# A hybrid attention block on one core: x and ctx transposed unscaled as half rows land, 1/rms spread over partitions, first-stage order pinned

## The chip, the cores and the metric

The kernel runs on one core of a Trainium2 chip. The metric is the device time of one execution in microseconds, shown as the median of three runs. All arithmetic is float32; a matmul operand is split into a high part (a float32 rounded to the matmul's own format, fp32r) and a low part, the remainder, so that one product becomes three matmuls.

## The reference

One layer of a backbone block with 256 latent tokens (`x`) and 256 context tokens (`ctx`), width 2048. What matters here is its beginning:

```python
sh1, sc1, ... = split(silu(c) @ w_mod + b_mod, 6)      # for x, from c
csh1, csc1, ... = split(silu(c_ctx) @ w_mod + b_mod, 6)  # for ctx, from c_ctx
h  = rmsnorm(x,   g_attn) * (1 + sc1)  + sh1
hc = rmsnorm(ctx, g_attn) * (1 + csc1) + csh1
cq, ckv, kr, qn, kn, vn, f   = split_columns(h  @ w_in)
cq_c, ckv_c, kr_c, ...       = split_columns(hc @ w_in)
```

where `rmsnorm(x, g)` is `x / sqrt(mean(x*x) + eps) * g` along a token's 2048 channels. Behind it follow three groups of attention and mixing heads, an output projection, and a gated MLP with a depthwise convolution.

## The kernel before

**Layout.** Token rows arrive with tokens on the 128 partitions: four tiles `xt[0..3]` of 128 tokens by 2048 channels, two of `x` and two of `ctx`. The first stage wants channels on partitions: `xT[m]` holds four channel blocks of 128 (kt = 4m to 4m+3) by 512 tokens.

**The start (lines 286 to 302 and 359 to 366).** SP issues the four loads of x and ctx, one of 1 MB each, and then the stream of weights. ScalarE issues the small loads: `sa` (modulation inputs), `sm` (among others the identity matrix for transposes, and `c` for `c1`) and `rope`. ScalarE then makes `c1` from `sm`, squares each x tile and sums it (`ssx`); VectorE and GpSimd (POOL) make 1/rms from that (`rstd`, lines 102 to 106), and VectorE multiplies the tile by it (line 301). TensorE transposes the scaled tile, four 128 x 128 blocks into one PSUM bank (line 364), with the identity from `sm`; VectorE and ScalarE take turns in copying the banks to `xT` (line 365).

**The first stage (lines 309 to 375).** For each of the 16 channel blocks kt there are two pieces of TensorE work. The *mod product* (`mod1_mm`, 32 matmuls of 256 columns, line 318) computes shift and scale of that block for both streams from 2 MB of `w_mod` (two tiles `m`); `mod1_h` transposes its copy `part` (line 326), VectorE finishes shift and scale in three small steps (lines 330 to 332), and VectorE and ScalarE make the modulated `hx` and `hc` with high and low parts (lines 342 to 344). The *group product* (`g1`, 42 matmuls, lines 109 to 111) adds that block's contribution to seven accumulators, from block `wA`, of which each 896 KB tile serves two kt in four quarters. The loop runs mod product g, the first `G1_CUT` tiles of group product g-1, `mod1_h(g)`, and the rest of g-1.

**Weights.** `emit_dma` issues loads on SP in the order of the list `order` (per pair of kt: m, m, A, m, m); tiles come from a pool of 16 buffers of 8 KB a partition, shared with x, `xT` and the squares' scratch. `take` splits quarters of a weight tile ahead of their use: `split` (lines 120 to 124) is a cast on ScalarE for the high part and a subtraction on VectorE for the low part.

**What sets the order.** A scheduler places each engine's instructions when the program is built; on the chip an engine runs them in that order, each waiting for the semaphores of what it needs. `tc.issue_after(i)` forbids the scheduler to place what follows before instruction i. An SP load waits for one of eight DMA semaphores, so about eight loads can be out at a time.

The lines that fill the start are these:

```python
act.activation(junk, xt[t], AF.Square, accum_out=ssx[:, t : t + 1])
rstd(rx[:, t : t + 1], ssx[:, t : t + 1], D)
dve.tensor_scalar(xt[t], xt[t], rx[:, t : t + 1], None, ALU.mult)
...
pe.transpose(ps[:, k * P : (k + 1) * P], xt[t][:, kt * P : (kt + 1) * P], ident)
```

## Time and profile before

| | |
|---|---|
| median of 3 runs | 1277.77 us (1277.18 to 1279.66) |
| profiled execution, its own time | 1279.01 us |
| its span, first to last instruction | 1277.2 us |
| TensorE busy | 1243.7 us, 97% of the span |
| VectorE, ScalarE, POOL busy | 77%, 55%, 9% |
| mean granted TensorE clock | 0.997 of full speed |
| moved by DMA | 304.81 MB, 239 GB/s on average |

The span is a little shorter than the execution's own time, which holds what lies before the first and behind the last instruction. Busy time is the sum of an engine's instructions; TensorE's weight loads are counted apart. Lines are those of the kernel before; tile names stand without their buffer numbers.

### The profile page before, as it was taken

To read this page: it belongs to the slowest core of one execution; us is meant where nothing else is said; L and a number is where in the kernel's file an instruction comes from. 1 tells how busy PE (TensorE), PEld (TensorE's weight loads), DVE (VectorE), ACT (ScalarE), POOL (GpSimd) and SP (SyncE) were. 2 spreads that over 40 slices of the span, in tenths; PEclk is the share of its full clock that TensorE was granted. 3 is DMA by queue.
4 is the path that set the end of the run, shared out by engine and by line. 5 is a ranking of instruction groups with operands and counts; after the bars stand their busy time and mean duration, and the time that the engine had idled before them with its cause. 6 is when DMAs were issued, how large, how long until landed. Compare 5 with 4: busy or idle time off the path is not lost.

```text
span 1277.2 us, 19956 instructions
## 1 busy us (share of the span) xinstructions
PE 1243.7 (97%) x7536; PEld 1069.2 (84%) x7536; DVE 978.6 (77%) x1757; ACT 699.0 (55%) x1343; POOL 111.5 (9%) x177
## 2 busy tenths in 40 slices
PE   5999999999999999999999999999999999999996
PEld 4888879898787888999988878888888888888885
DVE  5444588999989788899989975777766677777785
ACT  5333323765555555576666544666654566556663
POOL 0000121111111002200121500000000000000000
PEclk9999999999999999999999999999999999999999
DMA  9998689677756977754767857544455645564531
GB/s 387 419 397 327 223 305 323 231 243 249 258 194 232 368 294 270 261 227 165 286 226 253 320 204 264 212 162 169 165 198 180 249 165 183 184 227 165 172 125 66
DMA packets 53648, 304.81 MB, mean 239 GB/s; under 512 B 6064, under 2 KB 7216, under 8 KB 26800
## 3 DMA queue, kind: packets, MB, share of 16 engines
q1 hardware_dynamic: 34256, 234.37, 49.7%
q0 software_dynamic: 18432, 67.12, 15.5%
q10 hardware_dynamic: 864, 2.05, 0.4%
q8 instruction: 59, 0.97, 0.3%
q14 instruction: 37, 0.30, 0.1%
HBM read 301.42 MB, written 2.10 MB: 238 GB/s over the span
## 4 chain that ended last, share of the span: by engine, by line
PE 90%; DMA 3%; DVE 3%; issue 1%; ACT 1%; POOL 0%; DVEq 0%; ACTq 0%; POOLq 0%
PE ps L834 21%; PE ps L109 16%; PE ps L110 15%; PE ps L111 15%; PE ps L835 11%; DMA wm<-in_wm_dram 3%; PE g L109 2%; PE ms L318 2%; PE g L110 2%; PE g L111 2%; DVE acc L236 1%; DVE hl L124 1%; PE ps L493 1%; PE ps L364 1%; DMA sm<-in_small_dram 1%
## 5 line engine op out<-in xcount | busy, mean ns | idle before, releaser
L123 ACT CAST hl<-raw 128x512 fp32r<-128x512 f32 (+2 forms) x732 | 444.0, 611 | 359.8 <-PE ps L111 191.1
L124 DVE TENSOR_TENSOR hl<-raw,hl 128x512 fp32r<-128x512 f32 (+2 forms) x732 | 485.8, 677 | 172.6 <-ACT hl L123 166.4
L834 PE MATMUL ps<-hn,hl 128*128 128x512 f32 x1152 | 404.3, 395 | 0.0
L835 PE MATMUL ps<-hn,hl 128*128 128x256 f32 x1152 | 323.4, 281 | 0.0
L834 PEld LDWEIGHTS ps<-hn,hl 128*128 128x128 f32 x1152 | 216.4, 188 | 51.2
L835 PEld LDWEIGHTS ps<-hn,hl 128*128 128x128 f32 x1152 | 217.1, 188 | 0.2
L236 DVE SCALAR_TENSOR_TENSOR acc<-wm,c,acc 128x1024 f32<-128x1024 f32 x120 | 153.6, 1280 | 8.7 <-DMA wm<-in_wm_dram 8.4
L110 PE MATMUL ps<-hl,act 128*128 128x512 f32 x344 | 135.7, 394 | 0.5 <-DVE hl L124 0.5
L109 PE MATMUL ps<-hl,act 128*128 128x512 f32 x344 | 135.2, 393 | 0.0
L111 PE MATMUL ps<-hl,act 128*128 128x512 f32 x344 | 135.2, 393 | 0.0
L221 POOL DMA_DIRECT2D wm<-in_wm_dram x128 | 68.3, 534 | 310.7 <-DVE acc L236 233.8
L110 PEld LDWEIGHTS ps<-hl,act 128*128 128x128 f32 x344 | 64.7, 188 | 15.9 <-DVE hl L124 1.5
L109 PEld LDWEIGHTS ps<-hl,act 128*128 128x128 f32 x344 | 64.6, 188 | 14.9
L111 PEld LDWEIGHTS ps<-hl,act 128*128 128x128 f32 x344 | 64.7, 188 | 14.6
L109 PE MATMUL ps<-h,hl 128*128 128x258 f32 x256 | 72.5, 283 | 0.0
L111 PE MATMUL ps<-h,hl 128*128 128x258 f32 x256 | 72.1, 282 | 0.0
L110 PE MATMUL ps<-h,hl 128*128 128x258 f32 x256 | 72.1, 282 | 0.0
L216 POOL COPY hold<-hl 128x1 f32<-128x1 f32 x36 | 36.0, 999 | 286.7 <-DVE hl L124 286.7
L109 PE MATMUL ps<-hl,mix 128*128 128x512 f32 x128 | 50.5, 394 | 0.0
L110 PE MATMUL ps<-hl,mix 128*128 128x512 f32 x128 | 50.1, 391 | 0.0
L111 PE MATMUL ps<-hl,mix 128*128 128x512 f32 x128 | 49.9, 390 | 0.0
L855 ACT ACTIVATE cv<-ps,sm 128x256 f32<-128x256 f32 x88 | 49.4, 564 | 0.5
(282 smaller groups left out, 2143.2 us busy)
## 6 DMA issues: line engine op xcount, KB each, us to landing
raw<-in_wup_dram SPq DMA_DIRECT2D x88, 1024.0 KB, 5.1
wm<-in_wm_dram POOLq DMA_DIRECT2D x128, 512.0 KB, 5.1
raw<-in_wdn_dram SPq DMA_DIRECT2D x44, 1024.0 KB, 4.9
raw<-in_wm_dram SPq DMA_DIRECT2D x32, 1024.0 KB, 14.4
raw<-in_wo_dram SPq DMA_DIRECT2D x16, 1024.0 KB, 9.9
raw<-in_wB_dram SPq DMA_DIRECT2D x10, 1024.0 KB, 7.4
raw<-in_wA_dram SPq DMA_DIRECT2D x8, 896.0 KB, 14.5
x<-in_x_dram SPq DMA_DIRECT2D x4, 1024.0 KB, 8.8
```

Source lines behind the costliest of these rows:

```text
L109: pe.matmul(ps, lH, rH, start=first, stop=False, skip_group_check=skip)
L110: pe.matmul(ps, lH, rL, start=False, stop=False, skip_group_check=skip)
L111: pe.matmul(ps, lL, rH, start=False, stop=last, skip_group_check=skip)
L123: act.copy(H, src)
L124: return dve.tensor_tensor(L, src, H.bitcast(F32), ALU.subtract).ins
L216: hold = pool.tensor_copy(tiny(1, "hold"), recent[0][:, 1, 0:1].bitcast(F32)).ins
L221: pool.dma_start(w, a["wm2"][blk * 16 + kt])
L236: dve.scalar_tensor_tensor(m2["a"], w, c1[:, kt : kt + 1], m2["a"], ALU.mult, ALU.add)
L318: pe.matmul(ms[r : r + 32, 0:256], cs[:, 8 * q + k, :], w[:, k, :], start=(q == 0 and k < 4), stop=(q == 1 and k >= 4), tile_position=(0, r))
L834: pe.matmul(ps, w[:, 0, k * P : (k + 1) * P], h[:, :, k, :], start=kt == 0, stop=False, skip_group_check=True)
L835: pe.matmul(ps[:, :SEQ], w[:, 1, k * P : (k + 1) * P], h[:, 0, k, :], start=False, stop=kt == KT - 1, skip_group_check=True)
L855: act.activation(t, ps[:, :SEQ], AF.Identity, bias=c[:, 3:4], scale=c[:, 1:2])
```

## The change

The parts, in the order of the diff:

- `G1_CUT` is 2 instead of 4: `mod1_h` stands behind two tiles of the group product before, not four.
- The identity for the transposes, `idt`, is made on POOL from ones, and no longer read from `sm`.
- The load of a `wA` tile is cut into halves by columns; the second half is issued behind the next second mod tile.
- The quarters 2 and 3 of `wA` block 0 are split only behind the newest `hx`.
- x and ctx are loaded in eight half rows (512 KB each), then the first five weight loads are issued.
- `x_in`: per half row a Square with its own sum, and two groups of four transposes of the unscaled tile; all 16 copies to `xT` are on VectorE. `sm` is loaded behind the last Square.
- `x_rms`: the two half sums are added, 1/rms is made for all four tiles at once, put on a diagonal, and spread over all partitions by a product with ones, behind the first mod product; ScalarE copies it to `rxb`.
- `mod1_h` multiplies the block of `xT` by `rxb`, behind the h32 of the block before.
- Mod products and mod transposes of later blocks are held behind the group product issued before them; `rope` and `c1` stand behind the first `hx`.

```diff
-N_A, G1_CUT = 7, 4
+N_A, G1_CUT = 7, 2
...
+    idt = const.tile([P, P], F32, name="idt")
+    pool.affine_select(idt, ones, [[1, P]], ALU.is_equal, 0.0, base=0, channel_multiplier=-1)
...
-        pe.matmul(ps, lL, rH, start=False, stop=last, skip_group_check=skip)
+        ins = pe.matmul(ps, lL, rH, start=False, stop=last, skip_group_check=skip).ins
         paced(3 * rH.shape[-1])
+        return ins
...
             raw = b8([P, 2048], s="raw")
-            last_dma[0] = sync.dma_start(raw[:, :w], a[name][idx]).ins
+            if key[0] == "A":
+                sync.dma_start(raw[:, : w // 2], a[name][idx, :, : w // 2])
+                late_half.append((raw[:, w // 2 : w], a[name][idx, :, w // 2 :]))
+            else:
+                last_dma[0] = sync.dma_start(raw[:, :w], a[name][idx]).ins
+                if late_half and key[0] == "m" and key[2] == 1:
+                    sync.dma_start(*late_half.pop())
             raws[key] = raw
...
-            ins = split(t[:, 0, :hs], t[:, 1, :hs], raws[k][:, o : o + hs])
+            with ExitStack() as held:
+                if k == ("A", 0) and q >= 2:
+                    held.enter_context(tc.issue_after(hx_made[-1]))
+                ins = split(t[:, 0, :hs], t[:, 1, :hs], raws[k][:, o : o + hs])
             hls[k, q] = recent[0] = t
             last_split[0] = ins
...
+    ssrx = const.tile([P, 16], F32, name="ssrx")
+    ssx, sst, rx = ssrx[:, 0:8], ssrx[:, 8:12], ssrx[:, 12:16]
     xt = []
     for t in range(4):
         x_ = b8([P, D], s="x")
-        sync.dma_start(x_, (a["x"] if t < 2 else a["ctx"])[(t % 2) * P : (t % 2 + 1) * P, :])
+        for h in range(2):
+            sync.dma_start(x_[:, h * 1024 : (h + 1) * 1024],
+                           (a["x"] if t < 2 else a["ctx"])[(t % 2) * P : (t % 2 + 1) * P, h * 1024 : (h + 1) * 1024])
         xt.append(x_)
-        if t == 0:
+    emit_dma(order.index(("m", 1, 1)))
+    hmade, hx_made, g1_last, m_mm = [], [], [], []
+
+    def x_in():
+
+        last = None
+        for t in range(4):
+            junk = b8([P, D], s="junk")
+            for h in range(2):
+                c = slice(h * 1024, (h + 1) * 1024)
+                last = act.activation(junk[:, c], xt[t][:, c], AF.Square, accum_out=ssx[:, 2 * t + h : 2 * t + h + 1]).ins
+                for m in (2 * h, 2 * h + 1):
+                    ps = bank()
+                    for k in range(4):
+                        kt = 4 * m + k
+                        pe.transpose(ps[:, k * P : (k + 1) * P], xt[t][:, kt * P : (kt + 1) * P], idt)
+                    dve.tensor_copy(xT[m][:, :, t * P : (t + 1) * P], ps.rearrange("p (k q) -> p k q", k=4))
+        with tc.issue_after(last):
             act.dma_start(sm, a["small"])
-    act.dma_start(rope, a["rope"])
-    for t in range(4):
-        junk = b8([P, D], s="junk")
-        act.activation(junk, xt[t], AF.Square, accum_out=ssx[:, t : t + 1])
-        rstd(rx[:, t : t + 1], ssx[:, t : t + 1], D)
-        dve.tensor_scalar(xt[t], xt[t], rx[:, t : t + 1], None, ALU.mult)
-    act.activation(c1, smv("c1"), AF.Silu)
+
+    rxb = b2(s="rxb")
+
+    def x_rms():
+        sv = ssx.rearrange("p (t h) -> p t h", h=2)
+        dve.tensor_tensor(sst, sv[:, :, 0], sv[:, :, 1], ALU.add)
+        rstd(rx, sst, D)
+        dgs = b2(s="dgx")
+        dve.tensor_tensor(dgs.rearrange("p (t q) -> p t q", t=4), idt.rearrange("p (o q) -> p o q", o=1).broadcast_to((P, 4, P)),
+                          rx.rearrange("p (t o) -> p t o", o=1).broadcast_to((P, 4, P)), ALU.mult)
+        ps = bank()
+        with tc.issue_after(m_mm[0]):
+            pe.matmul(ps, ones, dgs, start=True, stop=True)
+        return act.copy(rxb, ps).ins
 
 
     hx, hc = [None] * 4, [None] * 4
...
     def mod1_mm(g):
 
-        for q in range(2):
-            w = raw_tile(("m", g, q), 6)
-            w = w.rearrange("p (k n) -> p k n", k=8)
-            for k in range(8):
-                r = 32 * (k % 4)
-                pe.matmul(ms[r : r + 32, 0:256], cs[:, 8 * q + k, :], w[:, k, :], start=(q == 0 and k < 4),
-                          stop=(q == 1 and k >= 4), tile_position=(0, r))
+        with ExitStack() as held:
+            if g:
+                held.enter_context(tc.issue_after(g1_last[-1]))
+            for q in range(2):
+                w = raw_tile(("m", g, q), 6)
+                w = w.rearrange("p (k n) -> p k n", k=8)
+                for k in range(8):
+                    r = 32 * (k % 4)
+                    ins = pe.matmul(ms[r : r + 32, 0:256], cs[:, 8 * q + k, :], w[:, k, :], start=(q == 0 and k < 4),
+                                    stop=(q == 1 and k >= 4), tile_position=(0, r)).ins
+                m_mm.append(ins)
         sb = b1(s="part")
         act.copy(sb, ms[:, 0:256])
         return sb
 
     def mod1_h(kt, sb):
-        for s in range(2):
-            pe.transpose(ms[:, 256 + s * P : 256 + (s + 1) * P], sb[:, s * P : (s + 1) * P], ident)
+        with ExitStack() as held:
+            if kt:
+                held.enter_context(tc.issue_after(g1_last[-1]))
+            for s in range(2):
+                pe.transpose(ms[:, 256 + s * P : 256 + (s + 1) * P], sb[:, s * P : (s + 1) * P], idt)
         t = tiny(4, "mt")
         tv = t.rearrange("p (s j) -> p s j", s=2)
...
+        xk = xT[m][:, kt % 4, :]
+        with ExitStack() as held:
+            if kt:
+                held.enter_context(tc.issue_after(hmade[-1]))
+            dve.tensor_tensor(xk, xk, rxb, ALU.mult)
...
-            dve.tensor_scalar(h32, xs, A, B, ALU.mult, ALU.add)
-            act.activation(H, xs, AF.Identity, bias=B, scale=A)
+            hmade.append(dve.tensor_scalar(h32, xs, A, B, ALU.mult, ALU.add).ins)
+            hx_made.append(act.activation(H, xs, AF.Identity, bias=B, scale=A).ins)
             dve.tensor_tensor(L, h32, H.bitcast(F32), ALU.subtract)
...
-            mm3(accs[i][:, SEQ:], lH, lL, *hsl(hc, kt), first=False, last=(kt == KT - 1), skip=True)
-
-    for t in range(4):
-        for m in range(4):
-            ps = bank()
-            for k in range(4):
-                kt = 4 * m + k
-                pe.transpose(ps[:, k * P : (k + 1) * P], xt[t][:, kt * P : (kt + 1) * P], ident)
-            (act.copy if m % 2 else dve.tensor_copy)(xT[m][:, :, t * P : (t + 1) * P],
-                                                     ps.rearrange("p (k q) -> p k q", k=4))
+            g1_last.append(mm3(accs[i][:, SEQ:], lH, lL, *hsl(hc, kt), first=False, last=(kt == KT - 1), skip=True))
+
+    x_in()
+    sb0 = mod1_mm(0)
+    rx_made = x_rms()
     accs = [bank(f"g1_{i}") for i in range(N_A)]
     for g in range(KT):
+        if g == 0:
+            mod1_h(0, sb0)
+            continue
+        if g == 1:
+            g1(0, range(0, 4))
+            with tc.issue_after(hx_made[-1]):
+                act.dma_start(rope, a["rope"])
+                act.activation(c1, smv("c1"), AF.Silu)
         sb = mod1_mm(g)
-        if g:
-            g1(g - 1, range(0, G1_CUT))
+        n = 5 if g == 1 else G1_CUT
+        g1(g - 1, range(4 if g == 1 else 0, n))
         mod1_h(g, sb)
-        if g:
-            g1(g - 1, range(G1_CUT, N_A))
+        g1(g - 1, range(n, N_A))
     g1(KT - 1, range(N_A))
```

Behind the first stage the instructions of every engine stand in the same order in both kernels. In it they move at three places. ScalarE's program, before, from its first activation; `junk` is a Square's scratch, `ps` a bank of transposes, `ms` the mod product, `raw_226` the tile of `wA` block 0, `hl` its split quarters:

```order
L99 ACTIVATE cs<-sa 128x16x2
L302 ACTIVATE c_75<-sm 128x16
L299 ACTIVATE junk_93,ssx<-x_83 128x2048
...
L299 ACTIVATE junk_111,ssx<-x_90 128x2048
L365 COPY xT_78<-ps_125 128x4x128
...
L321 COPY part_254<-ms_118 128x256
L123 CAST hl_296<-raw_226 128x512
L123 CAST hl_299<-raw_226 128x384
```

And in the changed kernel, where `raw_100` is that tile:

```order
L101 ACTIVATE cs<-sa 128x16x2
L126 CAST hl_275<-raw_100 128x512
L126 CAST hl_278<-raw_100 128x384
L318 ACTIVATE junk_109,ssrx<-x_84 128x1024 x2
...
L318 ACTIVATE junk_190,ssrx<-x_93 128x1024 x2
L326 DMA sm<-in_small_dram 128x552
L363 COPY part_240<-ms_108 128x256
L340 COPY rxb_107<-ps_248 128x512
L393 ACTIVATE hx_265<-xT_79,mt_260 128x256
```

The two casts of the first half of `wA` block 0 moved from behind the mod product's copy to ahead of the first Square; the activation of `c` and the copies to `xT` have left this stretch.

VectorE's program before, from the end of its memsets to the first split:

```order
L98 MEMSET cs 128x512
L105 TENSOR_SCALAR v_95<-ssx 128x1
L301 TENSOR_SCALAR x_83<-x_83,rx 128x2048
...
L365 COPY xT_77<-ps_119 128x4x128
...
L330 TENSOR_REDUCE mt_258<-ms_118 128x4
L331 TENSOR_TENSOR mt_258<-mt_258,sa 128x4
L332 SCALAR_TENSOR_TENSOR mt_258<-mt_258,sa 128x2
L342 TENSOR_SCALAR h_53_264<-xT_77,mt_258 128x256
...
L124 TENSOR_TENSOR hl_296<-raw_226,hl_296 128x512
```

And in the changed kernel, where `dgx` is the diagonal of 1/rms and `rxb` its spread:

```order
L100 MEMSET cs 128x512
L127 TENSOR_TENSOR hl_275<-raw_100,hl_275 128x512
L127 TENSOR_TENSOR hl_278<-raw_100,hl_278 128x384
L324 COPY xT_79<-ps_111 128x4x128
...
L324 COPY xT_82<-ps_211 128x4x128
L332 TENSOR_TENSOR ssrx<-ssrx 128x4
L107 TENSOR_SCALAR v_243<-ssrx 128x4
L375 TENSOR_REDUCE mt_260<-ms_108 128x4
L335 TENSOR_TENSOR dgx_246<-idt,ssrx 128x512
L376 TENSOR_TENSOR mt_260<-mt_260,sa 128x4
L377 SCALAR_TENSOR_TENSOR mt_260<-mt_260,sa 128x2
L383 TENSOR_TENSOR xT_79<-xT_79,rxb_107 128x512
```

The two subtractions of the same half moved ahead of all sixteen copies to `xT`, which stand here one behind the other; the steps to 1/rms moved behind the copies.

TensorE's program before, behind the transposes:

```order
L318 MATMUL ms_118<-raw_222,cs 32x256 x8
L318 MATMUL ms_118<-raw_224,cs 32x256 x8
L326 MATMUL ms_118<-sm,part_254 128x128 x2
L318 MATMUL ms_118<-raw_228,cs 32x256 x8
L318 MATMUL ms_118<-raw_230,cs 32x256 x8
L326 MATMUL ms_118<-sm,part_294 128x128 x2
L318 MATMUL ms_118<-raw_232,cs 32x256 x8
L109 MATMUL g_0_34_215<-hx_262,hl_296 128x256
```

And in the changed kernel:

```order
L359 MATMUL ms_108<-raw_96,cs 32x256 x8
L359 MATMUL ms_108<-raw_98,cs 32x256 x8
L371 MATMUL ms_108<-idt,part_240 128x128 x2
L339 MATMUL ps_248<-dgx_246,ones_r 128x512
L111 MATMUL g_0_43_251<-hx_265,hl_275 128x256
```

Before, two and a half mod products stand ahead of the first group product `g_0`; now there is one, and the product with ones. Before, two mod products also stand together at three later places of the stage (blocks 4, 8 and 12); now there are none such.

## Rows read from the trace of the kernel before

**Rows 1.** The page's chain that ended last: shares of the span by engine.

```profile
PE 90%; DMA 3%; DVE 3%; issue 1%; ACT 1%; POOL 0%; DVEq 0%; ACTq 0%; POOLq 0%
```

**Rows 2.** TensorE's waits, whole span: us in total, times, longest us.

```profile
PE ps L364 <- DVE v L105: 13.6, 1, 13.6
...
PE ps L270 <- ACT acl L123: 3.8, 2, 2.9
```

**Rows 3.** Timeline: start us, us, engine, line, operation, out<-in [idle before].

```profile
30.70 0.60 ACT L343 ACTIVATE hx<-xT,mt 128x256 fp32r<-128x256 f32 x1 [0.40 <-DVE mt L332]
...
31.33 0.74 PE L109 MATMUL g<-hx,hl 128*128 128x256 f32 x4
...
145.31 0.39 PE L109 MATMUL ps<-hl,hx 128*128 128x512 f32 x1
```

**Rows 4.** The chain in order of time: start us, us, what.

```profile
42.88 1.86 PE ms L318 x32
...
50.09 1.86 PE ms L318 x32
...
282.05 0.86 PE ps L461 x2
```

**Rows 5.** Windows: length, then busy us of PE, PEld, DVE, ACT, POOL; clock, DMA, GB/s.

```profile
31.00:146.00 115.00, 112.52 (x1143) 95.64 (x1136) 48.63 (x137) 37.96 (x78) 0.81 (x2) 1.00 0.89 350
58.50:62.00 3.50, 2.67 (x38) 1.31 (x27) 1.69 (x7) 2.55 (x6) 0.00 (x0) 1.00 1.01 422
```

**Rows 6.** Timeline of the start on ScalarE and VectorE.

```profile
9.34 0.22 ACT L302 ACTIVATE c<-sm 128x16 f32<-128x16 f32 x1 [1.67 <-DMA sm<-in_small_dram]
...
11.48 0.15 DVE L105 TENSOR_SCALAR v<-ssx 128x1 f32<-128x1 f32 x1 [9.92 <-ACT junk L299]
...
12.30 1.29 DVE L301 TENSOR_SCALAR x<-x,rx 128x2048 f32<-128x2048 f32 x1 [0.67 <-POOL rx L106]
```

**Rows 7.** DMA issues up to 20 us: count, KB each, us from issue to landing.

```profile
raw<-in_wA_dram SPq DMA_DIRECT2D x1, 896.0 KB, 15.5
...
sm<-in_small_dram ACTq DMA_DIRECT2D x1, 276.0 KB, 8.1
rope<-in_rope_dram ACTq DMA_DIRECT2D x1, 256.0 KB, 10.8
```

**Rows 8.** Timeline of SP: its issue of wA block 0.

```profile
6.47 0.45 SPq L173 DMA_DIRECT2D raw<-in_wA_dram  x1
```

**Rows 9.** The DMA view from 20 to 40 us.

```profile
DMA packets 1179, 8.42 MB, mean 421 GB/s; under 512 B 128, under 2 KB 128, under 8 KB 322
```

**Rows 10.** The page's DMA queues: packets, MB, share of 16 engines' span.

```profile
q1 hardware_dynamic: 34256, 234.37, 49.7%
q0 software_dynamic: 18432, 67.12, 15.5%
```

**Rows 11.** Timeline: copies to xT, and the splits of wA block 1.

```profile
20.15 3.08 DVE L365 COPY xT<-ps 128x512 f32<-128x512 f32 x5
...
35.38 1.97 ACT L123 CAST hl<-raw 128x512 fp32r<-128x512 f32 x4 [3.58 <-DMA raw<-in_wA_dram]
...
36.03 2.23 DVE L124 TENSOR_TENSOR hl<-raw,hl 128x512 fp32r<-128x512 f32 x4 [3.25 <-ACT hl L123]
```

**Rows 12.** Line 364 by stretches: ns min/median/max, first and last start us.

```profile
L364 PE MATMUL ps<-sm,x x12: 421/421/421, 15.6 to 18.0; 128*128 128x128 f32 x12
...
L364 PE MATMUL ps<-sm,x x20: 272/272/273, 19.8 to 21.9; 128*128 128x128 f32 x20
```

**Rows 13.** Windows behind TensorE's wait for acl, columns as in rows 5.

```profile
184.00:186.00 2.00, 1.92 (x5) 1.53 (x6) 2.00 (x5) 0.34 (x1) 0.00 (x0) 0.50 0.84 301
186.00:188.00 2.00, 2.00 (x8) 1.63 (x7) 2.00 (x3) 0.14 (x1) 0.54 (x1) 0.75 0.71 209
```

**Rows 14.** Groups by line and shape: busy us, mean ns, idle before.

```profile
L743 DVE TENSOR_TENSOR x<-x,tm 128x512 f32<-128x512 f32 x40 | 25.9, 685 | 0.1
L365 ACT COPY xT<-ps 128x512 f32<-128x512 f32 x8 | 4.6, 583 | 2.8 <-PE ps L364 2.8
```

More of the change, by code (lines that the diff above doesn't have):

```diff
@@ L145, in block_kernel @@
            "d": ("wdn", 2048)}
-    raws, hls = {}, {}
+    raws, hls, late_half = {}, {}, []
     recent, last_split, last_dma = [None], [None], [None]
@@ L286, in block_kernel @@
     xT = [b8([P, 4, 512], s="xT") for _ in range(4)]
-    ssx = const.tile([P, 4], F32, name="ssx")
-    rx = const.tile([P, 4], F32, name="rx")
+    ssrx = const.tile([P, 16], F32, name="ssrx")
+    ssx, sst, rx = ssrx[:, 0:8], ssrx[:, 8:12], ssrx[:, 12:16]
     xt = []
```

## The prediction

> **What bounds the kernel now.** I read the chain first: the reader is to see that TensorE makes 90% of it [rows 1]. Then TensorE's waits over the whole kernel: 13.6 us before the first transposes, and behind that nothing longer than 2.9 us [rows 2]. So no other engine has a cover that could swallow a shift: what TensorE gains or loses in the first stage moves the end by as much. Behind that stage every engine has the same order in both kernels, so I look only at the stage.
>
> Its length: the first group product starts at 31.33 us, the first product of the next stage at 145.31, 113.98 us apart [rows 3]. A mod product takes 1.86 us, and mod and group product together return every 7.21 us (42.88 to 50.09) [rows 4]. A window around one of the three places where two mod products stand together shows TensorE idle for 3.50 - 2.67 = 0.83 us [rows 5]; 2.5 us for three.
>
> The start: x has landed long before the first Square, but ScalarE stands at 9.34 behind a small activation that waits for `sm`, and the Squares behind it wait with it [rows 6]. An engine's queue stands behind its first waiting instruction: on that this forecast rests.
>
> **The change part by part.** Meant to be gained: the transposes need neither 1/rms nor `sm`, so they can start when half a row block is in, 0.5 MB or 1.25 us at 421 GB/s [rows 9] behind the first bytes at about 3 us: 4.5 instead of 13.65. But their results leave PSUM through VectorE alone, and in the new order two instructions stand there ahead of the first copy: the low parts of the first half of `wA` block 0. On ScalarE their two casts stand ahead of all eight Squares. Nothing pins these two quarters (only q >= 2 is held back).
>
> *When that half lands.* All of `wA` block 0 landed at 6.47 + 15.5 = 21.97 [rows 7, 8]. In the new order all of x and both halves of mod block 0 are still ahead of its first half; only `sm` (276 KB), `rope` (256 KB) and the second half of the block (448 KB), 1.0 MB, come later [rows 7]. At 421 GB/s [rows 9] that is 2.4 us: it lands at **19.6 us**. Half rows make smaller packets; the nearest rows are the POOL queue, with 3.6 KB a packet, 15.5% for 67.12 MB, and SP's, with 6.8 KB, 49.7% for 234.37, so 9% more per byte [rows 10]: x, 4.2 MB or 10 us, would cost 0.9 us more, or nothing. I take nothing; the engines were already full with larger packets.
>
> *The splits.* From the first cast to VectorE's first subtraction 0.65 us, four subtractions 2.23, so two 1.12 [rows 11]: VectorE is free at 21.4.
>
> *The copies.* Sixteen, none on ScalarE any more; five took 3.08 us back to back, 0.616 each [rows 11]: 9.9 us, to **31.3**. TensorE has filled the eight banks by then and stays ahead, with at worst 12 transposes in 2 us, 0.67 for a group of four [rows 12]: its last group ends near 27.5. The Squares: a copy of 512 columns takes ScalarE 0.58 [rows 14], so eight Squares of 1024 columns at most 9.3, from 20.7 to 30.0, not late.
>
> *Behind the copies* each step waits for the one before: the sum of the halves 0.2; from the mean's step to VectorE's instruction behind POOL's pow 0.82 (11.48 to 12.30) [rows 6]; the diagonal 0.69, like the product of the same size [rows 14]; the product with ones 0.86 [rows 4]; ScalarE's copy 0.58; x times 1/rms 0.69 [rows 14]; hx to the first group matmul 0.63 (30.70 to 31.33) [rows 3]. With five hand-overs of 0.05 this is 4.7, so the first group product starts at 31.3 + 4.7 = **36.0**, against 31.33.
>
> *What is left then.* Before, mod product 1 and half of 2 were done by then; now only product 0. So 1.5 mod products, 2.8 us, are added; the pinned order takes out the three double places, 2.5: 113.98 + 2.8 - 2.5 = 114.3. By the period alone it is 15 x 7.21 + 5.35 = 113.5, which I keep for the low end. The stage ends at 36.0 + 114.3 = 150.3, against 145.31: **5.0 us later**.
>
> *The clock.* Behind a wait of 2.9 us [rows 2] the granted clock was 0.50 for the stretch from 184 to 186 us (1.2 of 2.4 GHz), with 5 matmuls in it, and 0.75 in the next [rows 13]: 1.0 + 0.5 = 1.5 us lost. Between 29 and 36 TensorE now has only two short transposes and the product with ones, so the group products may begin slow: 0 to 1.5 us lost. I take 0.9, nearer to that row than to nothing. Before, the first transposes took 421 ns, and 272 later, with nothing but transposes ahead of them [rows 12]. The Trainium skill ("TensorE: Matmul & The Clock Gate", Part 4) says that transposes do not count as the activity that brings full clock; by that rule the time would be that of rival 3, but the row differs from it.
>
> *At no cost:* the multiplications by 1/rms, sixteen of 0.69 us, lie under the group products, where VectorE is busy 49 of 115 us [rows 5]; only the first is on the path, and counted. `sm` goes out behind the Squares, near 30, and took 8.1 us [rows 7], so it lands near 38, when `c1` on ScalarE wants it; behind that stand three casts and the copy of mod product 1, due near 40.8: if `sm` is 2 us late, about 0.6 us. The second halves of `wA` go out behind the next mod block, but are needed a period later.
>
> *Sum:* 5.0 + 0.9 = 5.9 us. The profiled execution took 1279.01 (span 1277.2), 1.2 above the median of 1277.77; I add the difference to the median: 1283.7, say **1284 us**.
>
> **The rivals.**
> 1. *Faster: the half of `wA` is not late.* If it overtakes x, the copies follow the half rows, and mod block 0, one `wA` half or 1.1 us ahead of 19.6, sets the pace: 18.5, 1.9 for its product, 0.9 for the copy and transposes, 0.7 for three small steps, 1.2 for hx and hand-overs: 23.2. The stage ends at 23.2 + 114.3 = 137.5, 7.8 us earlier: 1270. For it: nothing in the program holds that transfer behind x. Against it: with x, `sm`, `rope`, mod block 0 and itself, 7.8 MB, `wA` would land 18.6 us behind the first bytes, which is where it did land. The Trainium skill ("DMA: Bandwidth & Descriptors", Queues, rings and completion order) says that completion is not in order for one issuer; that rule would allow this rival, and no landing here shows it. Chance 0.05.
> 2. *No difference.* The low ends of the sum together give +4.2 (below); 1.7 us more are needed, as where the half lands that much earlier because the half rows start to flow sooner. Chance 0.08.
> 3. *The clock stays low through the whole start.* Mod product 0 takes 3.8 instead of 1.9 from 27.5 on, and its reduction stands ahead of the diagonal on VectorE: 0.4; the product with ones 0.9; the group products 1.5: 5.0 + 2.8 = 7.8, so 1285.6. The waits from 10 to 21 and 29 to 36 speak for it, the transposes between against it. Chance 0.15, inside slower.
> 4. *Much slower.* On ScalarE, casts that wait for a late half of `wA` stand ahead of the mod copy once in each of eight pairs; with each 1 us late it is 8 more: 1292. It decides only from where a half lands less than a mod product ahead of its use. Against it: the transfers' share over the stage is 0.89 [rows 5], so they have slack. Chance 0.07.
> The forecast itself has 0.65.
>
> **How the numbers follow.** Low end of the forecast: count by the period, -0.8, no clock loss, -0.9: +4.2, 1282. High end: late landing 0.9, clock 0.6, `sm` 0.6, reduction 0.4, ones 0.9: +9.3, 1287. With most of rival 2 and a margin for rival 4, the range is 1280.3 to 1288. A difference under 0.2%, 2.6 us, can't be told from none: 1275.2 to 1280.3. Faster 0.05, same 0.08, slower 0.87.
>
> **What would show it.** Right: ScalarE's first cast and VectorE's first subtraction near 19.6, ahead of every Square and xT copy; sixteen copies back to back to about 31; TensorE idle from about 10 to 22; the first group product near 36; no double mod products; the next stage near 150 to 152. Wrong: a first xT copy before 10 us (rival 1), a period other than 7.2 us (2, 4), or a wait behind the stage that shrinks by what the start loses.

## The result and the profile after

The changed kernel takes 1292.38 us (median of 6 runs, 1288.38 to 1293.67) against 1279.36 for the kernel before beside it, a ratio of 1.0098 (95% interval 1.0085 to 1.0111). A second series of the same kernel gave 1.0095 (1.0083 to 1.0108). So it is slower, as predicted, but by 13 us instead of 6; the predicted range ended at 1288.0. The profiled span went from 1277.2 to 1290.8 us.

First the chain that ended last in the changed kernel, by engine; TensorE makes 92% of it ([rows 1] before):

```profile
PE 92%; DMA 3%; DVE 2%; ACT 1%; issue 1%; POOL 0%; SPq 0%; DVEq 0%; POOLq 0%; ACTq 0%
```

TensorE's waits over the whole span (us in total, times, longest us), to be held against [rows 2]:

```profile
PE ps L323 <- DVE xT L324: 12.2, 1, 12.2
PE ps L323 <- DMA x<-in_x_dram: 5.2, 1, 5.2
PE ps L282 <- ACT acl L126: 4.6, 1, 4.6
PE g L111 <- ACT hx L393: 3.0, 2, 2.0
PE ps L339 <- DVE mt L376: 3.0, 1, 3.0
```

The one wait of 13.6 us has become two, 5.2 for the first half rows and 12.2 for a free bank, and three smaller ones follow, 3.0, 2.0 and, behind the stage, 4.6 instead of 2.9. The timeline of the changed kernel (start us, us, engine, line, operation, out<-in, idle before) shows why the 12.2 arises:

```profile
20.70 1.03 ACT L126 CAST hl<-raw 128x512 fp32r<-128x512 f32 x2 [13.82 <-DMA raw<-in_wA_dram]
21.36 1.16 DVE L127 TENSOR_TENSOR hl<-raw,hl 128x512 fp32r<-128x512 f32 x2 [19.74 <-ACT hl L126]
22.43 9.65 DVE L324 COPY xT<-ps 128x512 f32<-128x512 f32 x16
23.17 5.37 PE L323 MATMUL ps<-idt,x 128*128 128x128 f32 x32 [12.16 <-DVE xT L324]
28.47 1.93 PE L359 MATMUL ms<-raw,cs 128*32 128x256 f32 x32
32.44 1.03 POOL L108 TENSOR_TENSOR ssrx<-v,mhalf 128x4 f32<-128x4 f32 x1 [31.02 <-DVE mt L375]
34.34 2.04 PE L339 MATMUL ps<-dgx,ones_r 128*128 128x512 f32 x2 [3.00 <-DVE mt L376]
38.43 1.22 PE L111 MATMUL g<-hx,hl 128*128 128x256 f32 x4 [2.04 <-ACT hx L393]
43.80 1.93 PE L359 MATMUL ms<-raw,cs 128*32 128x256 f32 x32
155.58 0.40 PE L111 MATMUL ps<-hl,hx 128*128 128x512 f32 x1
```

The two casts of `wA` block 0 stand idle for 13.82 us until their half lands at 20.7; behind them VectorE has its two subtractions, and only then, at 22.43, the first of sixteen copies, 17 us after TensorE had the first transposes to give away. The first group product starts at 38.43 instead of 31.33 (+7.10), the first product of the next stage at 155.58 instead of 145.31 (+10.27) [rows 3]. The other 3.3 us of the 13.6 in the span are lost behind the stage.

Windows of the changed kernel (columns as in [rows 5]): the start, and the stretch behind the wait for `acl`, which answers to [rows 13]:

```profile
30.00:40.00 10.00, 4.46 (x19) 2.28 (x12) 6.25 (x17) 3.25 (x9) 1.03 (x1) 0.67 1.02 415
40.00:50.00 10.00, 10.00 (x103) 7.92 (x101) 5.54 (x14) 3.32 (x7) 0.00 (x0) 0.82 0.97 377
195.00:197.00 2.00, 2.00 (x4) 1.36 (x5) 2.00 (x4) 0.95 (x2) 0.08 (x1) 0.50 0.82 274
197.00:199.00 2.00, 2.00 (x6) 1.52 (x6) 2.00 (x4) 0.00 (x0) 0.53 (x1) 0.50 0.83 313
```

The granted clock is 0.67 and 0.82 up to 50 us, where TensorE idles and then begins the group products; behind the wait of 4.6 us it is 0.50 (1.2 of 2.4 GHz) in both windows, where before the second had 0.75. In windows of 1 us it stays at 0.50 until 200.7, 5.7 us behind the first `acl` product, and before until 187.0, 3.6 us behind it. `acl` is the split sum that VectorE accumulates for a later modulation, from weights `wm` that POOL loads.

### The profile page after: what moved, and what is told of

It is laid out like the page before. It is cut to its first block, busy times and chain, and to the rows that moved or that the text cites. A ratio compares the mean times of both kernels' runs of the same rounds, so it can differ in the third digit from the quotient of the medians.

```text
span 1290.8 us, 19980 instructions
## 1 busy us (share of the span) xinstructions
PE 1251.1 (97%) x7538; PEld 1076.6 (83%) x7538; DVE 987.1 (76%) x1776; ACT 695.6 (54%) x1344; POOL 112.2 (9%) x175
## 2 busy tenths in 40 slices
DMA packets 55378, 304.83 MB, mean 236 GB/s; under 512 B 6256, under 2 KB 7408, under 8 KB 29040
## 4 chain that ended last, share of the span: by engine, by line
PE 92%; DMA 3%; DVE 2%; ACT 1%; issue 1%; POOL 0%; SPq 0%; DVEq 0%; POOLq 0%; ACTq 0%
PE ps L886 21%; PE ps L111 17%; PE ps L112 16%; PE ps L113 16%; PE ps L887 11%; PE g L111 2%; PE ms L359 2%; PE g L112 2%; PE g L113 2%; DMA wm<-in_wm_dram 2%; DMA raw<-in_wA_dram 1%; PE ps L545 1%; DVE xT L324 1%; DVE acc L248 1%; PE ps L272 1%
```

## Experiments

The main theory: everything starts late because the half of `wA` block 0 stands ahead of the copies and the Squares (theory 1), and the clock then costs more (1a). The rivals: the copies themselves, which VectorE now makes alone (2); the pinned loop order (3). Each experiment was timed against the kernel before in five rounds; the table has all kernels, with three points of TensorE's timeline (us) from one profiled execution each.

| kernel | median, before beside it | ratio (95% interval) | first group product | first product of next stage | first acl product, its wait |
|---|---|---|---|---|---|
| before | | | 31.33 | 145.31 | 183.35, 2.9 |
| changed | 1292.38, 1279.36 | 1.0098 (1.0085 to 1.0111) | 38.43 | 155.58 | 194.96, 4.6 |
| e13_changed_again | 1292.46, 1279.95 | 1.0095 (1.0083 to 1.0108) | 38.28 | 154.53 | 191.62, 2.3 |
| e1_hold_split | 1283.96, 1280.55 | 1.0037 (1.0023 to 1.0052) | 26.14 | 147.96 | 186.27, 3.5 |
| e2_wa_first | 1282.61, 1280.55 | 1.0021 (1.0011 to 1.0031) | 33.49 | 150.37 | 188.50, 3.1 |
| e4_start_only | 1286.36, 1280.55 | 1.0060 (1.0044 to 1.0077) | 38.49 | 154.16 | 191.77, 2.6 |
| e5_order_only | 1277.01, 1280.55 | 0.9979 (0.9968 to 0.9990) | 29.61 | 142.84 | 182.43, 4.5 |
| e6_filled | 1289.73, 1280.02 | 1.0079 (1.0065 to 1.0094) | 38.56 | 153.22 | 191.97, 3.9 |
| e7_held_all | 1278.57, 1280.02 | 0.9991 (0.9981 to 1.0001) | 25.93 | 143.13 | 183.50, 5.5 |
| e8_seam | 1291.95, 1280.02 | 1.0097 (1.0080 to 1.0113) | 37.94 | 154.52 | 195.74, 6.4 |
| e9_gate_half | 1292.32, 1278.96 | 1.0101 (1.0085 to 1.0118) | 38.35 | 155.39 | 193.14, 3.0 |
| e10_start_filled | 1287.32, 1278.96 | 1.0063 (1.0049 to 1.0077) | 24.79 | 148.09 | 186.14, 3.0 |
| e11_start_gate | 1287.42, 1278.96 | 1.0063 (1.0050 to 1.0076) | 24.94 | 149.01 | 187.10, 3.1 |
| e12_start_held | 1278.56, 1279.95 | 0.9993 (0.9984 to 1.0002) | 24.81 | 141.40 | 180.85, 4.4 |

### The late half: e1_hold_split and e2_wa_first

The first takes the waiting instructions out of the two queues, the second makes them wait less:

```diff
-                if k == ("A", 0) and q >= 2:
-                    held.enter_context(tc.issue_after(hx_made[-1]))
+                if k == ("A", 0):
+                    held.enter_context(tc.issue_after(hx_made[-1] if q >= 2 else rx_made))
```

```diff
+    order.remove(("A", 0))
+    order.insert(0, ("A", 0))
```

> The changed kernel, but the casts and subtractions of the first half of wA block 0 are held behind the copy of the spread 1/rms, so nothing that waits for that half stands ahead of the Squares and the xT copies. Theory 1 (the half that lands at 20.7 sets the start): first xT copy before 7 us instead of 22.4, the last near 15; mod product 0 when its block lands, near 19.6; behind it part 0.6, transposes and reduction 0.8, diagonal 0.7, product with ones 0.9 to 2.0, copy 0.6, two casts 1.0, hx 0.6 and hand-overs: first group product at 27 to 29 (changed kernel 38.43), stage's end at 144 to 147 (155.58), 1278 to 1283 us. Theory 2 (the copies on VectorE alone are the limit): they still end near 26 or later, first group product not before 33, over 1286 us. Theory 3 (the pinned loop order costs the time): within 3 us of the changed kernel's 1292.4.

> The changed kernel, but the first half of wA block 0 is loaded ahead of the two halves of mod block 0 (2 MB, 5.0 us at 421 GB/s) instead of behind them. Theory 1: the first cast at 15.5 to 16.5 instead of 20.7, the sixteen copies end 4 to 5 us earlier, near 27.5, first group product near 33.8, and the whole kernel 4 to 6 us faster than the changed one: 1286.5 to 1288.5 us. Theory 2 (limit in the copies themselves, wherever they start): the same. Theory 3 (the loop order): within 1.5 us of 1292.4. Theory 4 (landings are not in order of issue, so the half lands when it lands): within 1.5 us of 1292.4.

The timeline of e2_wa_first:

```profile
15.77 1.03 ACT L126 CAST hl<-raw 128x512 fp32r<-128x512 f32 x2 [9.04 <-DMA raw<-in_wA_dram]
17.50 9.65 DVE L326 COPY xT<-ps 128x512 f32<-128x512 f32 x16
33.49 1.86 PE L111 MATMUL g<-hx,hl 128*128 128x256 f32 x7 [2.04 <-ACT hx L395]
150.37 0.40 PE L111 MATMUL ps<-hl,hx 128*128 128x512 f32 x1
```

The cast begins 4.93 us earlier, the copies 4.93, the first group product 4.94, the next stage 5.21: what the half lands earlier is handed on in full. That is theory 1. The copies take 9.65 us in both kernels, so they are a link of the chain but not what is late. The measured gain is larger than the stage shows and than the 4 to 6 us expected: 0.77% or 9.9 us. That comes up again below, with what lies behind the stage.

The timeline of e1_hold_split:

```profile
6.24 0.69 DVE L324 COPY xT<-ps 128x512 f32<-128x512 f32 x1 [4.62 <-PE ps L323]
26.14 1.86 PE L111 MATMUL g<-hx,hl 128*128 128x256 f32 x7 [2.10 <-ACT hx L393]
35.43 1.03 ACT L126 CAST hl<-raw 128x512 fp32r<-128x512 f32 x2 [5.64 <-DMA raw<-in_wA_dram]
37.56 0.54 PE L371 MATMUL ms<-idt,part 128*128 128x128 f32 x2 [3.18 <-ACT part L363]
147.96 0.40 PE L111 MATMUL ps<-hl,hx 128*128 128x512 f32 x1
```

The copies begin at 6.24, and the first group product comes 12.3 us earlier than in the changed kernel. But the stage ends only 7.6 earlier, and the expectations for its end and for the time are each missed by 1 us: now casts of `wA` block 1 stand ahead of the copy of mod product 1 on ScalarE, wait 5.64 us, and TensorE waits 3.18 for that copy. It is the prediction's fourth rival, in a kernel that reaches block 1 sooner than its half lands.

### The loop order: e4_start_only and e5_order_only

The first has the new start without the pins, the second the kernel before with the pins alone:

```diff
-N_A, G1_CUT = 7, 2
+N_A, G1_CUT = 7, 4
...
-                held.enter_context(tc.issue_after(g1_last[-1]))
```

```diff
-N_A, G1_CUT = 7, 4
+N_A, G1_CUT = 7, 2
...
+                held = tc.issue_after(g1_last[-1]) if g1_last else ExitStack()
```

> The changed kernel's start with the loop order of before: no pins on the mod products and their transposes, cut at 4. Mod product 1 then stands ahead of group product 0 again, two of the three double places are back, and one cast of wV is back ahead of the knH casts. Theory 1: mod product 1 is done in the wait before 38 us, which saves 1.9 us, two double places cost 1.7: the stage ends within 1 us of 155.6; if the longer acl wait behind the stage (4.6 against 2.9 us, with the half clock behind it 3.4 in all) hangs on that cast's place, the kernel is 3 to 4 us faster than the changed one, near 1288.5, and if it hangs on something else 1291 to 1293. Theory 3 (the loop order costs most of the 13 us): 1278 to 1283 us.

> The kernel before, with only the pinned order of mod and group products and the cut at 2. First group product at 31.3 as before or a part of a mod product earlier. Theory 1: the three double places go, each with 0.8 us, the stage ends 2 to 3.5 us earlier than 145.3; if the wait for acl behind it is not touched, 1275 to 1277 us; if the moved wV cast lengthens that wait as in the changed kernel (3.4 us with its half clock), 1278.5 to 1280. Theory 3 (the pinned order costs the time): 1285 us or more.

Of e5_order_only, the first group product and the first product of the next stage:

```profile
29.61 0.51 PE L109 MATMUL g<-hx,hl 128*128 128x256 f32 x2 [0.99 <-ACT hx L348]
142.84 0.39 PE L109 MATMUL ps<-hl,hx 128*128 128x512 f32 x1
```

The stage ends 2.47 us earlier than before, as the prediction reckoned for the three double places (2.5), and the kernel is 0.21% faster: in the kernel before, the pins gain. Its interval lies below 1, and of all kernels here it is the fastest. In e4_start_only the stage ends at 154.16, 1.4 us earlier than in the changed kernel's first profile and 0.4 earlier than in its second, since mod product 1 runs in TensorE's wait; 1.0060 against 1.0098 is 4.9 us, more than the stage shows and more than was expected, with intervals that do not overlap. So theory 3 falls as the main cause, but with the new start the pins cost time, and most of that behind the stage. That neither experiment alone tells: what the pins are worth depends on the start.

### The clock: e6_filled

```diff
+    def busy(n, behind, dst):
+        for i in range(n):
+            with tc.issue_after(behind):
+                behind = pe.matmul(dst, ones, cs.rearrange("p k j -> p (k j)"), start=True, stop=True).ins
+        return behind
```

> The changed kernel with matmuls that nobody uses (ones by a constant tile of 512 columns, 2 records each) in TensorE's waits of the start: ten before the last nine groups of transposes (wait of 12.2 us), four behind the transposes of mod product 0, two behind the product with ones. Theory 1a (the low clock of the start comes from the idle stretches, and costs 1.2 us in the product with ones and 2.6 in group product 0): these two take 0.9 and 2.8 us instead of 2.04 and 5.4, first group product near 37.3 instead of 38.43, the stage ends at 151.5 to 153 instead of 155.58, 3 to 4 us faster than the changed kernel, 1288 to 1289.5 us. Rival (the low clock is that of a start, whatever TensorE does): the same half clock to 43, first group product not earlier than 38.4, 1292 to 1294 us.

The timeline of e6_filled, TensorE alone:

```profile
11.15 8.75 PE L316 MATMUL ms<-cs,ones_r 128*128 128x512 f32 x20
32.07 3.60 PE L316 MATMUL ps<-cs,ones_r 128*128 128x512 f32 x8
35.50 1.02 PE L349 MATMUL ps<-dgx,ones_r 128*128 128x512 f32 x2
38.56 0.74 PE L111 MATMUL g<-hx,hl 128*128 128x256 f32 x4 [0.32 <-ACT hx L406]
41.59 1.93 PE L367 MATMUL ms<-raw,cs 128*32 128x256 f32 x32
153.22 0.40 PE L111 MATMUL ps<-hl,hx 128*128 128x512 f32 x1
```

Its window from 30 to 40 us, with the columns of [rows 5]:

```profile
30.00:40.00 10.00, 9.19 (x53) 4.71 (x45) 6.24 (x17) 3.24 (x10) 1.03 (x1) 1.00 1.02 418
```

With unused matmuls in the waits the clock is 1.00 instead of 0.67. From the first group matmul to mod product 1 it is now 3.03 us (38.56 to 41.59) instead of 5.37 (38.43 to 43.80), so the low clock cost 2.3 us there, and the stage ends 2.36 earlier (1.31 against the second profile of the changed kernel, below). The product with ones takes 1.02 instead of 2.04, but the unused matmuls ahead of it delay it by as much, so the first group product does not come earlier, and the half of the expectation that said so is missed. The measured ratio is 1.0079 against 1.0098, 2.4 us, with intervals that overlap; the expectation was 3 to 4. The rival, a low clock whatever TensorE does, falls by the granted clock and the 3.03 us.

### Behind the stage: e8_seam, e9_gate_half, e13_changed_again

The prediction said that behind the stage the order is the same. At the seam it is not quite: one cast of `wV` that stood ahead of the four casts of `knH` stands behind them in the changed kernel. e8_seam puts it ahead of two of them; e9_gate_half loads the gate's bias row in two halves, so that a `wm` load which VectorE waits for has less beside it:

```diff
+    look[0] = 5
+    hls[("V", 0), 0] = take(("V", 0), 0)
+    look[0] = 4
```

```diff
-            sync.dma_start(gates[blk // 6], a["bgate"][blk // 6 : blk // 6 + 1, :].broadcast_to((P, D)))
+        c = slice((blk % 2) * 1024, (blk % 2 + 1) * 1024)
+        with tc.issue_after(last_dma[0]):
+            sync.dma_start(gates[blk // 6][:, c], a["bgate"][blk // 6 : blk // 6 + 1, c].broadcast_to((P, 1024)))
```

> The changed kernel with one more cast of wV on ScalarE and VectorE moved back ahead of two of the four knH casts at the seam of the stages, as in the kernel before. Theory 1b (the wait for acl behind the stage is 4.6 instead of 2.9 us because that cast stands later, and the loads that are held behind it too): first acl product 37.5 to 38.3 us behind the first product of the next stage instead of 39.4, wait 2.6 to 3.3 us, 1289 to 1291 us. Rival (the wait follows the landing of one of the wm loads, which varies with what else is loaded, whatever that cast does): 38 to 39.6 us and 1291.5 to 1293.5 us.

> The changed kernel, but the gate's bias row (1 MB, issued some 20 us behind the stage's end) is loaded in two halves, each where its half is needed, the second some 20 us later. In every kernel so far the wm load that is under way beside it lands late, VectorE waits 2.0 to 5.1 us for it, and the acl wait of TensorE follows from that. Theory 1c (that load is late because of the gate's): VectorE's wait 4.6 falls to 2 to 3.4 us, first acl product 37 to 38.3 us behind the first product of the next stage (39.4), 1289 to 1291 us. Rival (late for another reason): 39 to 41 us, 1291.5 to 1293.5 us.

> The changed kernel once more, unaltered, for a second profile and a second ratio. If the 3.4 us that it lost behind the stage (wait for acl 4.6 us, half clock behind it) belong to the change, the second profile shows the acl product 39 us or more behind the stage's first product and the ratio is 1.009 to 1.011 again. If they belong to the single execution, the start (38.4) and the stage's end (155.6) come out within 0.5 us, and what lies behind differs by 1 us or more.

The first acl product in e8_seam, with the wait ahead of it:

```profile
195.74 0.80 PE L282 MATMUL ps<-acl,ones_r 128*128 128x512 f32 x1 [6.45 <-ACT acl L126]
```

The same in e9_gate_half:

```profile
193.14 0.50 PE L284 MATMUL ps<-acl,ones_r 128*128 128x512 f32 x1 [2.98 <-ACT acl L126]
```

And TensorE's timeline of e13_changed_again, from the first group product on:

```profile
38.28 1.22 PE L111 MATMUL g<-hx,hl 128*128 128x256 f32 x4 [2.03 <-ACT hx L393]
...
42.78 1.93 PE L359 MATMUL ms<-raw,cs 128*32 128x256 f32 x32
...
154.53 0.40 PE L111 MATMUL ps<-hl,hx 128*128 128x512 f32 x1
...
191.62 0.71 PE L282 MATMUL ps<-acl,ones_r 128*128 128x512 f32 x1 [2.32 <-ACT acl L126]
...
745.69 0.50 PE L112 MATMUL ps<-hl,act 128*128 128x512 f32 x1 [1.69 <-DVE hl L127]
```

With the cast moved forward the wait is 6.4, longer than without, and the ratio is 1.0097: theory 1b falls. With the gate's row in halves the wait is 3.0 in the profile, but the kernel is no faster (1.0101), and e11_start_gate below is no faster than e10_start_filled either: 1c gains no time. And the unaltered kernel had a wait of 2.3 in its second execution instead of 4.6, and yet from the stage's end to the end of the span 1289.7 - 154.53 = 1135.2 us, the same as in the first (1290.8 - 155.58 = 1135.2; before 1277.2 - 145.31 = 1131.9). The ratio came out as the first half of the expectation had it, the wait for acl as the second: what is lost behind the stage belongs to the change, but not to that wait.

TensorE's busy time shows where it is. Windows from the stage's end to the end of the span (columns as in [rows 5]), of the kernel before, the changed kernel and its second execution:

```profile
145.31:1277.20 1131.89, 1116.33 (x6258) 961.51 (x6256) 914.86 (x1589) 643.79 (x1239) 108.75 (x168) 1.00 0.63 223
155.58:1290.80 1135.22, 1119.41 (x6258) 964.12 (x6256) 914.56 (x1589) 642.44 (x1237) 110.22 (x168) 0.99 0.62 223
154.53:1289.70 1135.17, 1118.85 (x6258) 963.10 (x6256) 914.79 (x1589) 642.49 (x1237) 104.90 (x168) 1.00 0.63 223
```

TensorE is not busy for 15.6, 15.8 and 16.3 us of them, so the waits together are hardly longer; its busy time is 3.1 and 2.5 us longer, for the same 6256 matmuls. One group of the last stage shows it, on the pages of the kernel before and the changed one (busy us, mean ns, idle before):

```profile
L834 PE MATMUL ps<-hn,hl 128*128 128x512 f32 x1152 | 404.3, 395 | 0.0
L886 PE MATMUL ps<-hn,hl 128*128 128x512 f32 x1152 | 405.8, 396 | 0.0
```

Matched one by one, the times from one matmul's start to the next differ from those of the kernel before. Differences of at most 20 ns add up to 2.5 us in both executions, those at waits of more than 0.35 us to 0.7 and 0.8. Between the two executions 4655 of the 6255 times are equal to the nanosecond, between the kernel before and the changed one 955: these small differences belong to the program and not to the execution. They are 2.4 to 2.5 us in e1_hold_split, e8_seam and e9_gate_half too, -0.8 in e2_wa_first, 1.8 in e4_start_only, -0.5 in e5_order_only, 3.9 in e12_start_held and 4.9 and 5.0 in e10_start_filled and e11_start_gate. That explains a part of what e2 gains beyond its stage. What sets them is open: no run changed that alone.

### The start mended: e7_held_all, e10_start_filled, e11_start_gate, e12_start_held

e7_held_all holds the splits of all `wA` blocks behind the `hx` before them and pulls the product with ones forward. e10_start_filled adds unused matmuls at the start and holds only blocks 0 and 1; e12_start_held holds 0 to 4; e11_start_gate is e10_start_filled with the halves of e9_gate_half.

```diff
-                if k == ("A", 0) and q >= 2:
-                    held.enter_context(tc.issue_after(hx_made[-1]))
+                if k[0] == "A" and k[1] < 5:
+                    held.enter_context(tc.issue_after(rx_made[0] if k[1] == 0 and q < 2 else hx_made[-1]))
...
+                if g == 0 and q == 1:
+                    m_mm[0] = busy(FILL[1], m_mm[-1], fill_bank[0])
+                    rx_made.append(x_rms())
```

> As e1_hold_split, and further: the splits of every wA block are held behind the hx of the mod product before, so that no late cast stands ahead of the copy of a mod product on ScalarE (in e1_hold_split mod product 1's copy stood behind three casts that waited 5.6 us for wA block 1); the diagonal stands ahead of the reduction on VectorE, and the product with ones between the two halves of mod product 0. Theory 1 (order on ScalarE ahead of late halves is what costs): first group product at 23 to 25 (26.14 in e1_hold_split), no wait of 3 us for the copy of mod product 1, stage's end at 138 to 142, 1270 to 1275 us. Rival (by then the loads themselves are the limit: at 421 GB/s a period's 2.6 MB take 6.1 us, and mod blocks 1 and 2 land just before they are due): waits for the mod blocks, half clock again, stage's end at 143 to 147, 1277 to 1283 us.

> The start of e7_held_all with the clock kept up: unused matmuls (two behind the last transposes, one before and one behind the product with ones, two behind the transposes of mod product 0), the casts of wA block 0 right behind the copy of 1/rms, and only wA blocks 0 and 1 held. Theory 1 with 1a: first group product at 23.5 to 25 instead of 25.93, its 24 matmuls in 2.8 instead of 5 us, the wait of 2.0 us for a held cast gone, stage's end at 138.5 to 141 instead of 143.13, 1273 to 1276.5 us. Rival (behind the stage the acl chain, fed by the loads, takes back what the stage gains): stage's end as said, first acl product not before 182.5, 1277 to 1279 us. Second rival (loads of mod blocks limit): stage's end not before 142.5.

> e10_start_filled with the gate's bias row in halves as in e9_gate_half. Theory 1c: 1 to 2.5 us faster than e10_start_filled, by an acl wait that is that much shorter. Rival: no difference to e10_start_filled.

> e10_start_filled, but wA blocks 0 to 4 are held behind the hx of the mod product before, not only 0 and 1: in e10_start_filled mod product 3's copy stood 7.3 us behind two casts that waited for wA block 2, TensorE waited 4.8 us and fell to half clock. Theory 1 (a late half of wA ahead of a mod copy on ScalarE costs 5 to 8 us wherever it stands): that wait goes, first group product near 24.8, stage's end at 139.5 to 141.5 instead of 148.1, 6 to 8 us faster than e10_start_filled's 1287.3: 1277 us by what lies behind the stage in e10_start_filled's profile, 1274 by what lies behind it before. Rival (another wait takes its place, for a mod block or a later half of wA): stage's end not before 144, 1281 us or more.

The timeline of e10_start_filled, first ScalarE, then TensorE:

```profile
48.12 1.03 ACT L126 CAST hl<-raw 128x512 fp32r<-128x512 f32 x2 [7.29 <-DMA raw<-in_wA_dram]
49.06 0.36 ACT L376 COPY part<-ms 128x256 f32<-128x256 f32 x1
...
49.48 0.68 PE L384 MATMUL ms<-idt,part 128*128 128x128 f32 x2 [4.83 <-ACT part L376]
...
148.09 0.40 PE L111 MATMUL ps<-hl,hx 128*128 128x512 f32 x1
```

TensorE's timeline of e12_start_held:

```profile
24.81 0.41 PE L111 MATMUL g<-hx,hl 128*128 128x256 f32 x1
...
141.40 0.39 PE L111 MATMUL ps<-hl,hx 128*128 128x512 f32 x1
...
180.85 0.80 PE L282 MATMUL ps<-acl,ones_r 128*128 128x512 f32 x1 [4.42 <-ACT acl L126]
```

The window behind that wait, with the columns of [rows 5]:

```profile
181.00:187.00 6.00, 6.00 (x14) 4.39 (x15) 5.25 (x8) 1.46 (x3) 1.05 (x2) 0.50 0.84 277
```

e10_start_filled misses its expectation by 7 us in the stage and by 11 in the time, and shows the fault a third time: block 2 is not held, its casts wait 7.29 us ahead of the copy of mod product 3, and TensorE 4.83. All that e12_start_held changes is that hold; the wait is gone and the stage ends 6.7 us earlier, the kernel is 0.70% or 9.0 us faster. That settles theory 1: taking casts that wait for a late half of `wA` from ahead of what is needed next on ScalarE gained 7.6 us of the stage's end in e1_hold_split and 6.7 here; in e1 itself the next such place took back 4.7 (12.3 less 7.6), together with whatever else separates its first group product from its stage's end.

e12_start_held ends the stage 3.9 us earlier than the kernel before, and e7_held_all 2.2; yet at the end 0.1% is left, and both intervals hold 1. In the profile of e12_start_held the gain is gone at the end: from the stage's end on it takes 1278.0 - 141.40 = 1136.6 us, 4.7 more than before. There is a longer wait for acl in it (4.4 for 2.9, with the half clock for 6 us behind it), but TensorE is not busy for 15.8 us in all, as before, and 3.9 of the 4.7 are the small differences. Both kernels are slower than expected (1270 to 1275, and 1274 to 1277). e7_held_all also ends its stage 1 us later than the 138 to 142 expected, inside its rival's range; but of the waits that the rival names its trace has one of 1.42 us, for mod block 0, beside 2.27 for `hx` and, near 118 us, 1.99 for a held split. That the loads are the limit is not shown.

## Why the prediction was right in direction and wrong in size

**Right.** The mechanism held: the first cast and the first subtraction ahead of every Square and copy, sixteen copies in a row, no double mod products, a period near 7.2 us in all but one place. Rival 1 fell: the half landed behind all that was issued before it, and issued ahead of 2 MB (5.0 us at 421 GB/s) its cast began 4.93 earlier. By the rule of the Trainium skill on completion order ("DMA: Bandwidth & Descriptors", Queues, rings and completion order) it could have overtaken; no landing of SP's loads at this start did. Rival 3 fell in its first term: mod product 0, right behind the transposes, took 1.93 us, as at full clock [rows 4], and not 3.8. Its terms for the product with ones (0.9) and the group products (1.5) came true, and more: 1.2 and up to 2.3 us. Here too the trace does not bear out what the Trainium skill says of PE-mode transposes, that they do not bring full clock ("TensorE: Matmul & The Clock Gate", Part 4): the granted clock was 0.50 when the second half of the transposes began at 23.17 and 1.00 from 26.6 on, with nothing but transposes between. Rival 4 did not strike the changed kernel, which is too late for it, but it struck e1_hold_split, e10_start_filled and e11_start_gate, which start much sooner and leave later blocks unheld.

**Wrong in the start, 2.4 us.** The first group product came at 38.43, not 36.0. The landing, *19.6*, was 20.7 (1.1): I took nothing for the smaller packets and had 0.9 as the other end. In the three windows of 2 us from 2 to 8 us DMA moved 219, 391 and 330 GB/s, where before it was 302, 414 and 416; that is 0.38 MB, or 0.9 us at 421 GB/s. But from 8 to 12 us, with half rows still landing, it moved 408 and 424, so that the packets' size is the reason is not shown. The copies were 0.3 shorter than reckoned. The steps *behind the copies*, 4.7, took 6.35 (32.08 to 38.43): the product with ones ran at half clock, 2.04 for 0.86 [rows 4], and POOL's pow on four columns took 1.03 us instead of the 0.55 (shown at the end) that lay in the 0.82 of [rows 6]. The row for the pow was one on 128x1, and I did not scale it.

**Wrong in the clock, 1.4 to 0.6 us.** Group product 0 lost 2.3 us to the low clock by e6_filled, in its second execution 1.5 (38.28 to 42.78, less 3.03), and I took 0.9. The row I leaned on, the stretch behind the wait for acl [rows 13], shows a shorter idle time than the one here, where TensorE had been idle for 12.2 us and twice for 2 to 3. The stage from first group product to its end, reckoned at 114.3 without the clock, took 117.15 - 2.3 = 114.8; the half microsecond more lies within the one longer period, 8.35 us from 127.68 to 136.03, where TensorE waits 0.99 us for `hx` at 130.60.

**Wrong behind the stage, 3.3 us.** *What TensorE gains or loses in the first stage moves the end by as much* failed, and it is the largest of the errors. From the stage's end to the end of the span it is 1131.9 us before and 1135.2 in both profiles of the changed kernel, but 1129.1 in e2_wa_first (1279.5 - 150.37) and 1136.6 in e12_start_held. The prediction took the same order of instructions for the same time. The order is the same but for one cast and its subtraction; the time of the same 6256 matmuls is not, and 2.5 of the 3.3 us are differences of at most 20 ns from one to the next. The waits for `acl`, whose accumulations on VectorE are fed by loads of their own, vary from 2.3 to 6.4 us at the first place and have 3.5 to 6 us of half clock behind them where I looked, but in all they make up less than 1 us of the difference. What sets the small differences stays open. The order at the seam and the gate's load were tried and are not it.

One reading of the start was loose, at no cost: *x has landed long before the first Square* holds for the first tile only (landed at 5.9 us, its Square at 9.46); the last tile of ctx landed at 14.7, and its Square began at 15.14.

So of 13.6 us in the span 10.3 come from the stage, where the runs show the cause: the late half (e1, e2, e10 against e12) and the clock behind the idle start (e6). The other 3.3 are located, in TensorE's products behind the stage, but not explained. The direction did not hang on luck: the late first group product alone costs 7.1 us.

## What to carry to other kernels

Before work is moved to an idle start, list for each engine what stands ahead of it and when the data of that lands; an instruction that is early in the order and late in its data holds back the whole queue, and mending the first place uncovers the next. The same order of instructions behind a change does not promise the same time: here what followed took 1129.1 to 1136.7 us. Profile an unaltered kernel twice before a wait is blamed, and compare TensorE's busy time with its idle time: the wait that looked guilty varied by 2 us while the total stayed the same. Behind an idle stretch, reckon the first products at half clock for as long as the rows nearest in idle time show, not for the shortest of them.

## What the runs showed of the hardware

POOL's pow of two operands took 1.03 us on 128x4; in the kernel before it took half of that on 128x1:

```profile
11.72 0.55 POOL L106 TENSOR_TENSOR rx<-v,mhalf 128x1 f32<-128x1 f32 x1 [11.27 <-DVE v L105]
```

Unused matmuls in TensorE's waits kept the granted clock at 1.00 from 30 to 40 us in e6_filled, and the group product behind them gained 2.3 us; ahead of the product with ones they cost as much as its full clock saved. And the landing of a load followed the bytes issued ahead of it closely: moved ahead of 2 MB, its cast began 4.93 us earlier, where 421 GB/s give 5.0. The times from one matmul's start to the next were nearly the same in two executions of the changed kernel (4655 of 6255 equal to the nanosecond), and against the kernel before they differed by a few ns each, 2.5 us in all behind the stage.
